# One small operation of block 2's heads, and the copies of the second inverse, get another place in the order

## The chip, the cores and the metric

The kernel runs on one core of a Trainium2 chip. The metric is the device time of one execution in microseconds (us), the median of several runs. Traces come from one profiled execution each. TensorE is called PE, VectorE DVE, ScalarE ACT, GpSimd POOL and SyncE SP; SP issues nearly all DMAs of this kernel, from one queue in order.

## The reference

Two transformer-like blocks over 1024 tokens of width 1024, all in float32. Block 1 (an RWKV branch, a short convolution, a pooling branch) is not touched. Block 2 puts 16 learned meta tokens ahead of the 1024, projects the normalized rows, and then has

- a Fourier branch: a two-dimensional transform over time and channels, and a gate;
- a delta-rule branch with 8 heads of 128 channels. Queries, keys and values go through a depthwise convolution of 5 taps and a SiLU. With the running sum `g` of log decays inside a chunk, `decay[c, s] = exp(g[c] - g[s])` for `s <= c`, and `A = strict_lower((beta*k) k^T * decay)`. `T = (1 + A)^-1` is a unit triangular inverse. The state recurrence over the chunks uses `T`, `q`, `k`, `v` and `decay`, forward and backward in time; the output is normalized per head, multiplied by `silu(z)` and projected;
- a hierarchical mixture of experts.

In code, the core of the part that the change touches:

```
a_mat = where(strict, einsum("bhncd,bhnsd->bhncs", k_beta, k) * decay, 0)
t_mat = triangular_solve(eye + a_mat, eye, lower=True, unit_diagonal=True)
qk    = where(lower, einsum("bhncd,bhnsd->bhncs", q, k) * decay, 0)
```

## The kernel before

The 1040 rows of block 2 are the 16 meta tokens (the meta chunk) and 8 chunks of 128 tokens. A matmul in near-float32 precision is three passes (`mm3`, lines 195 to 197) with both operands split into a high and a low part. Weights stream through `WStream.get`: a 512 KB load (line 184), the high part by ACT (line 172), the low part by POOL (line 173).

**The heads.** The loop at the end of the heads' section runs over 8 heads. For each it projects and convolves the keys, queries and values (`channels`: three projections of three pieces each; PE, ACT copies at line 991, five taps at lines 997 and 999, SiLU at line 1000). Between the pieces it runs one step of the previous head's generator `head`, so the small work of head h-1 lies between the projections of head h. That small work, in the order of the code:

- `token_rows`: transposes of keys and queries (lines 1017 and 1027) into PSUM tiles called "m", of which there are two; ACT squares them (line 1029, tile `jk`), DVE sums the squares (line 1030), ACT copies the rows out (line 1033);
- `decay_matrices(h, 0)`: from `gb`, the rows of `g` broadcast to all partitions, eight DVE operations of 128x128 (line 1090: four chunks, two directions), then ACT's exponential (line 1092). The tiles `dm0` and `dm1` have two buffers each;
- `value_rows`: transposes of the values (lines 1055 and 1063), also through "m";
- `gram_meta`: for the meta chunk a 16x16 product (line 1076, into "m"), one small DVE operation on `gb` (line 1078), its exponential on ACT (line 1080), the product of both on DVE (line 1081), a store (line 1082);
- `decay_matrices(h, 1)` for the other four chunks, and `gram` twice (lines 1105 to 1123), whose products are multiplied with the decays and stored for the inverses.

`decays_in(h)` loads `gb` for both directions (line 1006, 576 KB each, two buffers each) from the scratch `GR`, which `gates_b` has written from a DVE copy (line 974) and a store (line 975).

**What sets the order.** The kernel is traced in the order of the code; a planner then simulates it with estimated durations and puts each engine's instructions into a fixed order: of those that its simulation says are ready, the ones traced earlier first. On the chip each engine follows its order and waits at semaphores. `tc.issue_after(ins)` gives every instruction traced in its block on `ins`'s engine an edge that puts it behind `ins` in that engine's order; it adds no semaphore, and instructions of other engines in the block get no edge. `rows_of[0]` holds such an instruction: the last `GR` copy of `gates_b`, behind which each head's `decay_matrices(h, 0)` stands.

**The inverses.** Behind the heads DVE solves two triangular inverses of 128 matrices of 64x64 (lines 421 and 423), the second one backwards (`solve1`, in place in the tile named `tab`), interleaved with the Fourier branch and its gates. `z_gate(h)` projects the gate of a head and applies SiLU (line 1190, two halves). `inverse_out` stores the inverse (line 1230) and, in four copies by ACT (line 1233, two buffers) with a store each (line 1234), its transpose. After that come nine halves of `gate_d` (line 1373) and the loop over the chunks, which reads both.

Of the kernel before, what the change touches and what calls it, by code (L numbers as in the profile page):

```python
# [17 lines left out]
OP = mybir.AluOpType  # L18
# [109 lines left out]
def tile_kernel(tc, A):  # L128
    with ExitStack() as ctx:
        body(ctx, tc, A)  # L130


def body(ctx, tc, A):
    nc = tc.nc
    act, dve, pool_e, pe, sp = nc.scalar, nc.vector, nc.gpsimd, nc.tensor, nc.sync
# [148 lines left out]
    with ExitStack() as ca:  # L284
# [30 lines left out]
        for pr in range(4):  # L315
# [6 lines left out]
            for half in range(2):  # L322
# [36 lines left out]
                def c8(x):  # L359
# [10 lines left out]
                                         op0=OP.mult, op1=OP.mult)  # L370
# [13 lines left out]
                for g in range(2):  # L384
# [5 lines left out]
                    c = half * 8 + 4 * g  # L390
# [8 lines left out]
                for g in range(2):  # L399
                    c = half * 8 + 4 * g  # L400
# [52 lines left out]
    with ExitStack() as ci:  # L453
        pi = sb("pi", 1, ci)
        X = pi.tile([P, 64, 64], F32, name="X")
        t = pi.tile([P, 1024], F32, name="t")
# [22 lines left out]
    with ExitStack() as cs:  # L479
# [4 lines left out]
        for c in range(16):  # L484
# [38 lines left out]
            if c % 2 == 1:  # L523
                i = c // 2
# [91 lines left out]
    for dt in range(4):  # L616
# [8 lines left out]
        for half in range(2):  # L625
# [3 lines left out]
            for i in range(2):  # L629
                dve.scalar_tensor_tensor(y[half], cu[:, i + t0:512 + i + t0], cw[:, i, dt:dt + 1], y[half],  # L630
                                         op0=OP.mult, op1=OP.add)
# [244 lines left out]
    def con2(name):  # L876
        o, n = cols2.at[name]
        return C2[:, o:o + n]
# [14 lines left out]
    gc = c2.tile([P, 2, 9, H], F32, name="gc")  # L893
# [18 lines left out]
    with ExitStack() as cg:  # L912
# [66 lines left out]
        KQs_, vs_, sks, gbs, silus, rows_of = {}, {}, {}, {}, [None], [None]  # L979
# [92 lines left out]
        def gram_meta(h):  # L1072

            KQ, gb = KQs_[h], gbs[h][0]
            q = psm.tile([P, 4, P], F32, name="m")
            pe.matmul(q[:16, 0, :16], KQ[:, 0, 0:16], KQ[:, 0, 0:16], start=True, stop=True)
            dm = pg.tile([16, 16], F32, name="dmm", bufs=4)
            dve.scalar_tensor_tensor(dm, gb[:16, 0, :16], gc[:16, 0, 0, h:h + 1],
                                     con2("dmf")[:16, :16], op0=OP.subtract, op1=OP.min)
            act.activation(dm, dm, AF.Exp)  # L1080
            dve.scalar_tensor_tensor(dm, q[:16, 0, :16], nbp[:16, 0, 0, h:h + 1], dm, op0=OP.mult, op1=OP.mult)
            sp.dma_start(NM[h], dm)

        def decay_matrices(h, gq):
            grb, dm = gbs[h], []
            for d_ in range(2):
                t = pg.tile([P, 4, P], F32, name=f"dm{d_}", bufs=2)
                for i in range(4):
                    c = 1 + 4 * gq + i
                    dve.scalar_tensor_tensor(t[:, i], grb[d_][:, c, :], gc[:, d_, c, h:h + 1],  # L1090
                                             con2("dmf" if d_ == 0 else "dmb"), op0=OP.subtract, op1=OP.min)
                act.activation(t, t, AF.Exp)
                dm.append(t)
            return dm

        def gram(h, gq, dm):
# [30 lines left out]
        def head(h):  # L1127
            yield from token_rows(h)
            with tc.issue_after(rows_of[0].ins):
                dm0 = decay_matrices(h, 0)  # L1130
            yield from value_rows(h)
            gram_meta(h)
            yield
            dm1 = decay_matrices(h, 1)
            yield from gram(h, 0, dm0)
            yield from gram(h, 1, dm1)
# [49 lines left out]
    def z_gate(h):  # L1186
        w = win2.get(3584 + h * P)
        for half, tt in enumerate(HALF):
            t = pz.tile([P, 512], F32, name="z")
            gated[0] = act.activation(t, half2(w, half), AF.Silu)  # L1190
            sp.dma_start(Z2[h * P:(h + 1) * P, tt], t)
# [37 lines left out]
    def inverse_out(d_, X):  # L1229
        sp.dma_start(TS2[d_], X)  # L1230
        for i in range(4):
            t = pi.tile([P, 16, 64], F32, name="t", bufs=2)
            act.activation(t, X[:, :, 16 * i:16 * i + 16].rearrange("p s t -> p t s"), AF.Copy)
            sp.dma_start(TN2[d_, :, 16 * i:16 * i + 16, :], t)
# [88 lines left out]
    ones(X1_)  # L1323
    for h in range(5, H):
        z_gate(h)
        if h == 5:
            with tc.issue_after(gated[0].ins):
                inverse_out(1, X1_)
    cpi.close()
# [313 lines left out]
    with ExitStack() as ce:  # L1643
# [133 lines left out]
        for half in range(2):  # L1777
            if half:
                ready += [expert_raw(e, whole(weo, 2), parts=early) for e in range(2)]
                for _ in delta_half(1, big, pf, 2):  # L1780
                    if later:
                        i, f = later.pop(0)
# [41 lines left out]
    with ExitStack() as ce:  # L1824
# [11 lines left out]
        for i in range(2):  # L1836
            t = pm.tile([P, D], F32, name=f"xg{i}", bufs=1)
# [357 lines left out]
```

## Time and profile before

| | |
|---|---|
| median of 3 runs | 3046.23 us (3042.31 to 3051.17) |
| profiled execution | 3044.02 us, span 3042.3 us |
| mean granted PE clock | 0.964 |
| PE busy | 2781.8 us (91%), 16109 matmuls |
| weight loads (PEld) busy | 2230.4 us (73%) |
| DVE busy | 1518.0 us (50%) |
| ACT busy | 1027.7 us (34%) |
| POOL busy | 888.6 us (29%) |
| block 2's heads | about 1250 to 1613 us |
| inverses, Fourier branch, gates | about 1613 to 1960 us |

A line of a timeline gives the start in us, the duration in us, the engine, the source line, the operation, output and inputs with shapes, the count, and in brackets how long the engine had been idle before it and what ended that wait. "q" and "m" are PSUM tiles. The granted clock is a share of the full 2.4 GHz. What ended a wait is inferred from semaphores, the last to come being named.

### The profile page before, as it was taken

The page shows a single profiled execution, that of the slowest core. Times are in us where ns is not written, and L with a number is a line of the kernel's source. Part 1 is how long each engine was busy: PE and PEld are TensorE (multiplying, and loading weights), DVE is VectorE, ACT ScalarE, POOL GpSimd, SP SyncE. Part 2 cuts the span into 40 slices and gives each one's busy share as a digit, 9 for nine tenths or more (in the row PEclk, how much of TensorE's full clock was granted, in tenths as well). Part 3 has the DMA queues.
Part 4 walks back from the last instruction along what each step waited for, and adds up shares of the span by engine and source line. Part 5 has one row for each costly group of instructions (what it writes and reads, how often), then busy time and mean ns, then how long its engine had stood idle before and what let it go on. Part 6 is the DMA issues. An engine that isn't in the chain of part 4 may idle for free. (4 is left out here: it accounts for less than half of the span.)

```text
span 3042.3 us, 42743 instructions
## 1 busy us (share of the span) xinstructions
PE 2781.8 (91%) x16109; PEld 2230.4 (73%) x16109; DVE 1518.0 (50%) x2516; ACT 1027.7 (34%) x1837; POOL 888.6 (29%) x703
## 2 busy tenths in 40 slices
PE   7999999999999998798999999999999986888884
PEld 6777877888788787798898778789888753545442
DVE  3343993324411345565677989633564442222226
ACT  5444112223322334565673222244543210111112
POOL 1333223223233552111114852222475310111011
PEclk9999999999999999999999999999999988999997
DMA  4456514544244354466553334599988569999996
GB/s 119 122 141 181 181 42 142 153 134 131 80 137 149 120 149 123 106 154 142 140 145 118 117 94 136 160 275 260 264 248 296 195 248 401 416 404 412 400 370 281
DMA packets 532929, 599.77 MB, mean 197 GB/s; under 512 B 120784, under 2 KB 429188, under 8 KB 512368
## 3 DMA queue, kind: packets, MB, share of 16 engines
q1 hardware_dynamic: 525808, 582.60, 59.2%
q0 software_dynamic: 6912, 14.41, 1.3%
q8 instruction: 128, 2.10, 0.3%
q14 instruction: 81, 0.66, 0.1%
HBM read 473.23 MB, written 134.44 MB: 200 GB/s over the span
## 5 line engine op out<-in xcount | busy, mean ns | idle before, releaser
L173 POOL TENSOR_TENSOR wl<-wr,wh 128x1024 fp32r<-128x1024 f32 x142 | 367.0, 2585 | 632.0 <-ACT wh L172 624.0
L196 PE MATMUL q<-hTh,wl 128*128 128x512 f32 x1040 | 412.8, 397 | 8.0 <-POOL wl L173 8.0
L195 PE MATMUL q<-hTh,wh 128*128 128x512 f32 x1040 | 416.3, 400 | 2.3 <-DVE t L824 1.4
L197 PE MATMUL q<-hTl,wh 128*128 128x512 f32 x1040 | 416.7, 401 | 0.0
L195 PE MATMUL q<-h2h,wh 128*128 128x346 f32 (+4 forms) x1080 | 389.2, 360 | 5.9 <-ACT wh L172 3.4
L196 PE MATMUL q<-h2h,wl 128*128 128x346 f32 (+4 forms) x1080 | 383.3, 355 | 1.6 <-POOL wl L173 1.6
L197 PE MATMUL q<-h2l,wh 128*128 128x346 f32 (+4 forms) x1080 | 381.3, 353 | 0.0
L196 PEld LDWEIGHTS q<-hTh,wl 128*128 128x128 f32 x1040 | 196.6, 189 | 57.7 <-POOL wl L173 9.5
L195 PEld LDWEIGHTS q<-hTh,wh 128*128 128x128 f32 x1040 | 196.6, 189 | 50.4 <-issue 5.8
L197 PEld LDWEIGHTS q<-hTl,wh 128*128 128x128 f32 x1040 | 196.7, 189 | 46.3 <-issue 3.9
L195 PEld LDWEIGHTS q<-h2h,wh 128*128 128x128 f32 (+1 forms) x1080 | 206.7, 191 | 26.6 <-ACT wh L172 3.8
L196 PEld LDWEIGHTS q<-h2h,wl 128*128 128x128 f32 (+1 forms) x1080 | 206.3, 191 | 20.6 <-POOL wl L173 2.1
L197 PEld LDWEIGHTS q<-h2l,wh 128*128 128x128 f32 (+1 forms) x1080 | 205.8, 191 | 18.4 <-issue 0.2
L438 DVE TENSOR_TENSOR t<-X 128x62 f32<-128x62 f32 (+30 forms) x124 | 155.5, 1254 | 10.8 <-DMA br<-in_w_branch_dram 7.7
L172 ACT ACTIVATE wh<-wr 128x1024 fp32r<-128x1024 f32 x142 | 148.5, 1046 | 36.2 <-PE q L197 16.8
L440 DVE TENSOR_TENSOR X<-X,t 128x62 f32<-128x62 f32 (+30 forms) x124 | 151.0, 1218 | 2.8
L1843 POOL DMA_INDIRECT xg<-HN,gidx x28 | 28.6, 1022 | 373.6 <-PE t L1856 313.4
L1862 PE MATMUL q<-yl,xT 128*32 128x256 f32 (+2 forms) x416 | 107.4, 421 | 26.3 <-DMA yl<-in_w_gate_e_dram 26.0
L1864 ACT ACTIVATE sg<-q 128x256 f32<-128x256 f32 x28 | 10.8, 384 | 325.2 <-PE q L1862 325.2
L1862 PE MATMUL q<-mh,xT 128*64 128x256 f32 (+2 forms) x416 | 107.0, 417 | 11.8 <-DMA mh<-in_w_gate_e_dram 11.5
L1865 DVE TENSOR_TENSOR sg<-sg,q 128x256 f32<-128x256 f32 x28 | 11.8, 421 | 211.1 <-ACT sg L1864 211.1
L1862 PE MATMUL q<-g,xT 128*32 128x256 f32 (+2 forms) x400 | 88.0, 449 | 25.4 <-DMA g<-in_w_gate_e_dram 23.4
(631 smaller groups left out, 5890.8 us busy)
## 6 DMA issues: line engine op xcount, KB each, us to landing
wr<-in_w_in_dram SPq DMA_DIRECT2D x125, 512.0 KB, 4.7
d<-in_w_down_e_dram SPq DMA_DIRECT2D x38, 1024.0 KB, 17.6
g<-in_w_gate_e_dram SPq DMA_DIRECT2D x25, 1024.0 KB, 20.0
u<-in_w_up_e_dram SPq DMA_DIRECT2D x25, 1024.0 KB, 17.7
KQ<-KQs SPq DMA_DIRECT2D x32, 512.0 KB, 7.2
KV<-KVs SPq DMA_DIRECT2D x32, 512.0 KB, 6.2
wr<-in_w_gate_e_dram SPq DMA_DIRECT2D x26, 512.0 KB, 18.7
mh<-in_w_gate_e_dram SPq DMA_DIRECT2D x13, 1024.0 KB, 13.7
```

The costliest lines, as they stand in the source:

```text
L172: act.activation(hi, src, AF.Copy)
L173: pool_e.tensor_sub(lo, src, hi.bitcast(F32))
L195: pe.matmul(out, sh(k), mh(k), start=(k == 0), stop=False)
L196: pe.matmul(out, sl(k), mh(k), start=False, stop=False)
L197: mm[0] = pe.matmul(out, sh(k), ml(k), start=False, stop=(k == kt - 1))
L438: dve.tensor_tensor(t, X[:, 0:s, s:s + 1].to_broadcast([X.shape[0], s, m]), X[:, s:s + 1, s + 1:n].to_broadcast([X.shape[0], s, m]), op=OP ...
L440: dve.tensor_add(X[:, 0:s, s + 1:n], X[:, 0:s, s + 1:n], t)
L1843: nc.gpsimd.indirect_dma_start(out=xg, out_offset=None, in_=HN, in_offset=bass.IndirectOffsetOnAxis(ap=gi, axis=0), bounds_check=S - 1, oo ...
L1862: up[0] = pe.matmul(qs[r_, j], xT[:, k, r_], w[j][k], start=(k == 0), stop=(k == 7))
L1864: si[0] = act.activation(sg, qs[:, 0], AF.Silu)
L1865: dve.tensor_mul(sg, sg, qs[:, 1])
```

## The change

Two edits. First, the small DVE operation of `gram_meta` stands behind the last large decay operation traced before it, which is the eighth of `decay_matrices(h, 0)`. For that, `decay_matrices` now writes its last operation into `rows_of[0]`; so the block around `decay_matrices(h, 0)` in `head` stands, from the second head on, behind the last operation of `decay_matrices(h-1, 1)`, no longer behind the `GR` copy. Second, `inverse_out(1, X1_)` is traced in the last turn of the gates' loop, after `z_gate(7)`, and its ACT copies stand behind that gate's second SiLU; before, it was traced after `z_gate(5)` and behind that gate's.

```diff
-            dve.scalar_tensor_tensor(dm, gb[:16, 0, :16], gc[:16, 0, 0, h:h + 1],
-                                     con2("dmf")[:16, :16], op0=OP.subtract, op1=OP.min)
+            with tc.issue_after(rows_of[0].ins):
+                dve.scalar_tensor_tensor(dm, gb[:16, 0, :16], gc[:16, 0, 0, h:h + 1],
+                                         con2("dmf")[:16, :16], op0=OP.subtract, op1=OP.min)
             act.activation(dm, dm, AF.Exp)
...
                 for i in range(4):
                     c = 1 + 4 * gq + i
-                    dve.scalar_tensor_tensor(t[:, i], grb[d_][:, c, :], gc[:, d_, c, h:h + 1],
-                                             con2("dmf" if d_ == 0 else "dmb"), op0=OP.subtract, op1=OP.min)
+                    rows = dve.scalar_tensor_tensor(t[:, i], grb[d_][:, c, :], gc[:, d_, c, h:h + 1],
+                                                    con2("dmf" if d_ == 0 else "dmb"), op0=OP.subtract, op1=OP.min)
                 act.activation(t, t, AF.Exp)
                 dm.append(t)
+            rows_of[0] = rows
             return dm
...
         z_gate(h)
-        if h == 5:
+        if h == 7:
             with tc.issue_after(gated[0].ins):
                 inverse_out(1, X1_)
```

## Rows read from the trace of the kernel before

**Rows 1.** Waits of PE, 1180 to 1620 us: total, times, longest.
```profile
PE m L1063 <- ACT jk L1029: 36.0, 6, 11.7
PE m L1027 <- DVE jk L974: 5.8, 1, 5.8
```
**Rows 2.** Waits of all engines, 1300 to 1600 us.
```profile
DVE dmm L1078 <- DMA gb<-GR: 54.6, 5, 12.0
```
**Rows 3.** Timeline of DVE, around one stalled head.
```profile
1313.22 1.14 DVE L1090 SCALAR_TENSOR_TENSOR dm<-gb,gc,C 128x128 f32<-128x128 f32 x4
...
1330.25 0.22 DVE L1078 SCALAR_TENSOR_TENSOR dmm<-gb,gc,C 16x16 f32<-16x16 f32 x1 [10.23 <-DMA gb<-GR]
...
1339.29 0.22 DVE L1081 SCALAR_TENSOR_TENSOR dmm<-m,nbp,dmm 16x16 f32<-16x16 f32 x1 [1.61 <-PE m L1076]
...
1397.80 2.20 DVE L1090 SCALAR_TENSOR_TENSOR dm<-gb,gc,C 128x128 f32<-128x128 f32 x8
```
**Rows 4.** Timeline of ACT, the same head.
```profile
1330.51 0.21 ACT L1080 ACTIVATE dmm<-dmm 16x16 f32<-16x16 f32 x1 [7.14 <-DVE dmm L1078]
```
**Rows 5.** Timeline of PE, the same head.
```profile
1332.65 0.94 PE L1063 MATMUL m<-ident,v 128*128 128x128 f32 x4 [4.92 <-ACT jk L1029]
...
1333.68 0.49 PE L196 MATMUL q<-h2h,wl 128*128 128x346 f32 x1
...
1336.61 0.32 PE L195 MATMUL q<-h2h,wh 128*128 128x346 f32 x1
```
**Rows 6.** Busy time by stretch, cut at decay groups; stretch, length, engines, clock, DMA share, GB/s.
```profile
1303.03:1350.62 47.59, 42.66 (x261) 41.60 (x260) 29.97 (x68) 30.90 (x50) 8.88 (x10) 0.96 0.67 148
1350.62:1397.80 47.18, 42.71 (x261) 41.59 (x261) 29.97 (x68) 30.93 (x50) 8.88 (x10) 0.96 0.61 147
1397.80:1445.17 47.37, 42.70 (x258) 41.64 (x257) 29.98 (x68) 30.38 (x50) 8.90 (x10) 0.93 0.62 146
1445.17:1493.28 48.11, 43.29 (x264) 42.20 (x263) 30.15 (x69) 31.24 (x51) 8.92 (x10) 0.93 0.57 144
1493.28:1541.82 48.54, 43.09 (x263) 41.98 (x263) 29.99 (x68) 31.33 (x51) 8.90 (x10) 0.93 0.59 143
1541.82:1581.90 40.08, 40.08 (x257) 39.28 (x256) 30.52 (x67) 28.95 (x49) 8.89 (x10) 1.00 0.51 138
1249.80:1312.01 62.21, 44.77 (x267) 43.36 (x266) 33.48 (x83) 31.74 (x56) 7.62 (x10) 0.89 0.49 129
```
**Rows 7.** Timeline of DVE, heads 0 to 2.
```profile
1257.98 0.22 DVE L1078 SCALAR_TENSOR_TENSOR dmm<-gb,gc,C 16x16 f32<-16x16 f32 x1 [6.89 <-DMA gb<-GR]
1258.13 0.27 DVE L974 COPY jk<-m 72x128 f32<-72x128 f32 x1
...
1274.75 0.88 DVE L1090 SCALAR_TENSOR_TENSOR dm<-gb,gc,C 128x128 f32<-128x128 f32 x3 [7.58 <-DMA gb<-GR]
```
**Rows 8.** Timeline of SP's queue, heads 0 to 2.
```profile
1249.86 5.27 SPq L184 DMA_DIRECT2D wr<-in_w_in_dram  x1
...
1265.62 7.04 SPq L1006 DMA_DIRECT2D gb<-GR  x3
```
**Rows 9.** Timelines of ACT and PE, heads 0 to 2.
```profile
1277.56 0.63 ACT L1092 ACTIVATE dm<-dm 128x512 f32<-128x512 f32 x1 [0.42 <-DVE dm L1090]
1283.85 0.21 ACT L1080 ACTIVATE dmm<-dmm 16x16 f32<-16x16 f32 x1 [5.66 <-DVE dmm L1078]
...
1284.93 1.12 PE L1063 MATMUL m<-ident,v 128*128 128x128 f32 x4 [11.66 <-ACT jk L1029]
```
**Rows 10.** Instructions of lines 1190 and 1233; then PE's timeline behind the copies.
```profile
L1190 ACT ACTIVATE z<-q x16: 580/598/605, 1648.2 to 1915.3; 128x512 f32<-128x512 f32 x16
...
L1233 ACT ACTIVATE t<-tab x4: 1911/2010/2054, 1946.6 to 1956.7; 128x1024 f32<-128x1024 f32 x4
...
1951.98 0.79 PE L195 MATMUL q<-h2h,wh 128*128 128x512 f32 x1 [3.40 <-ACT wh L172]
...
1954.39 0.80 PE L196 MATMUL q<-h2h,wl 128*128 128x512 f32 x1 [1.62 <-POOL wl L173]
```

## Prediction

> **What bounds the kernel now.** I began with the granted clock and the page's forty slices: TensorE (PE) is busy for nine tenths of nearly every slice, so a change is worth what it does to PE's few gaps. The waits of PE over block 2's heads name them: two causes, the value transposes of line 1063 six times (36.0 us, the longest 11.7) and one transpose of line 1027 (5.8) [rows 1]. PE is said to wait there for ScalarE's squares (line 1029), which says who came last, not why. The timelines of the other engines say why. VectorE stands still before the meta chunk's decay operation (line 1078), 54.6 us in five heads, until the load of the row-broadcast decays `gb` lands [rows 2]. For head 3: VectorE finished reading the buffer's former contents in the group at 1313.22, the next load could only then start, and the meta operation reached the front of VectorE's queue 10.23 us before that load had landed at 1330.25 [rows 3]. ScalarE had its exponential (line 1080) at the front of its own queue and idled 7.14 us, until 1330.51 [rows 4]. The squares and PSUM copies behind it could not release the two "m" buffers, so PE idled 4.92 us before 1332.65, and then ran a matmul of 346 columns in 0.49 us where it takes 0.32 at the higher clock, until about 1336.6 [rows 5].
>
> The urgent reader of `gb` is thus the smallest one. The 128x128 decay operations of the same head come at 1397.80 for head 3 (eight of them, the first half of the head's decays), 67 us after its `gb` had landed [rows 3].
>
> **First edit, heads 3 to 7.** Afterwards the meta operation stands behind the last large decay operation of its own head's first half, which reads the same `gb`. Nothing is added to the work: 0.22 us on VectorE and its exponential on ScalarE move. The price of the stall is read from a natural comparison. Cut the trace at the start of each head's first eight decay operations, and each stretch is one head's period. Five periods hold one stalled meta operation each (heads 3 to 7) and last 47.59, 47.18, 47.37, 48.11 and 48.54 us. The sixth holds none, because there is no ninth head whose meta operation could stand there, and lasts 40.08 us with PE busy for all of it at clock 1.00 [rows 6]. The differences are 7.51, 7.10, 7.29, 8.03 and 8.46, in all 38.4 us. They split into PE idle (span minus busy: 4.93, 4.47, 4.67, 4.82, 5.45; 24.3) and PE busier than 40.08 by 2.58 to 3.21 (14.1), which is the lower clock after each gap.
>
> Is the sixth period fair as a model? It has no `gb` loads. The DMA share of the five is 0.57 to 0.67 of 47.2 to 48.5 us, at most 31.9 us of the DMA engines' time, which in 40.08 us is a share of 0.80: it fits. I take no loss; as a bound I take the spread of the five periods, 1.4 us, for each of five, 7 us.
>
> Who is late next: in the sixth period nobody before PE. VectorE is busy 30.5 and ScalarE 29.0 of 40.08 us, and the moved 0.22 us goes beside PE. The meta product (line 1081) needs the moved result only at 1339.29 for head 1, whose first eight decay operations began at 1303.03 (the first cut); so the result still comes over 30 us early [rows 3, 6].
>
> The edit also resets the handle that the next head's first decays are ordered behind (once the copy of `GR`, now the second half of the head before). In the trace they stand in that order already: head 1's second half ends near 1314.4, head 2's first half starts at 1350.62, where the second stretch is cut [rows 3, 6]. Cost 0.
>
> **First edit, heads 0 to 2.** Here the stall is mixed with the start of the stage. From the first value-convolution tap of head 0 to that of head 1 takes 62.21 us [rows 6], 22.1 above 40.08. Meta 0 waits until 1257.98 for the first `gb`, and behind it the copy for the second direction's `GR` runs only at 1258.13 [rows 7]. Without the meta operation that copy runs some 7 us sooner, but the next thing on VectorE, head 0's large decays, waits for the same load. SP was still issuing a weight load from 1249.86 for 5.27 us, and the second direction's loads could only go at 1265.62, to be waited for until 1274.75 [rows 7, 8]. I count nothing for this, since that load cannot be shown to come earlier. What surely goes is meta 2: ScalarE finished its large exponentials at 1278.2 (1277.56 plus 0.63) and then idled 5.66 us until the meta's exponential at 1283.85; PE's 11.66 us gap ended at 1284.93, a square and a copy later [rows 9]. PE can resume 5.7 us sooner. Bounds: 0 (the load is later still) and 22.1 (the whole excess). I take 5.7, because it is one instruction's wait read from its row, while the rest hangs on loads.
>
> **Second edit.** The copies of the second inverse are to follow the eighth gate's second Silu. In the trace they do: the last of the 16 Silus starts at 1915.3, the first of those four copies at 1946.6 [rows 10]. The planner has put them behind three activations of the next gate as well, and they wait for VectorE's solve. The edge asks for nothing new. Their trace position falls behind the weight splits, loads and Silus of two gates that all run earlier anyway. What lies on the SP queue behind the inverse's own store is in the same order. So 0. Bounds: if the copies did move, PE's gap of 3.40 + 1.62 us, in which the weight split waits behind the first copies, could go (gain 5.0); or the four copies of 2.01 us each (8.0) could come late for the chunk loop that reads them (loss 8.0).
>
> **The sum.** 38.4 + 5.7 + 0 = 44.1 us off the profiled execution's 3044.0 (span 3042.3) is 2999.9. That execution lies 2.2 below the median of the three runs, 3046.2, so the forecast on that footing is 3002. I take the work behind the heads to move earlier as a block.
>
> **Rivals.**
> 1. *Only the idle time returns.* PE at full duty would keep the lower clock for as many matmuls. Gain 24.3 + 5.7 = 30.0, time 3016. Against it: the sixth period, 40.08 us busy throughout, shows 1.00, and the slow matmuls of head 3 follow its gap [rows 5, 6]. The Trainium skill ("TensorE: Matmul & The Clock Gate", Part 1: The HAM clock gate) says that for a model the penalty of the clock's ramp is under 1% of a typical kernel's span; left out on that ground, it gives this rival's sum. So it is here too as a share of the span, but it is 14.1 of the 38.4 us that these heads can give back, too much to leave out. Chance 0.08.
> 2. *The wait passes on.* With the meta operation gone, another reader of `gb` comes to the front while the load is under way, or the planner, which knows nothing of the real landing time, pulls another operation there. Time about 3046. For it: one large decay operation did wait, at 1274.75 [rows 7]. Against: from head 3 on they come 67 us after the landing, since their own output buffers hold them back until the products before them are done. Chance 0.06.
> 3. *More than counted.* The start of the stage runs at the sixth period's pace and the gap at the copies closes: 38.4 + 22.1 + 5.0 = 65.5, time 2981. For it: the earlier `GR` copy. Against: the loads it feeds stand behind others. Chance 0.07.
> 4. *Slower.* The meta product frees one of the two "m" PSUM buffers, and now depends on the large decays through VectorE's order. If the planner lets PE's meta matmul go before those decays, PE loses a buffer until they are done: from a meta product at 1339.29 to the end of the next decay group (1350.62 and eight operations of about 0.28, 1352.8) is 13.5 us, for eight heads 108, less the 44.1 saved: 64 slower, 3110. It begins where the decays come after their head's meta matmul; for head 1 they come over 30 us before its product, and the code writes them before it. Chance 0.05.
>
> **How the numbers follow.** The forecast has 0.74. Its own range is 2992 to 3012: 7 us for the DMA bound, and the runs' own spread of about 5 each way. To hold 8 in 10 I reach to rival 1 and part of the way to rival 3: 2986 to 3020. A difference under 0.3% (9 us) can't be told from none. Faster: forecast, rivals 1 and 3, 0.89. Same: rival 2, 0.06. Slower: rival 4, 0.05.
>
> **What would show it.** Right: line 1078 no longer waits for `gb` in VectorE's waits; PE has no gap at line 1063 in heads 3 to 7; every period between first decay groups is 40 to 41.5 us at clock 1.00; near the start one PE gap remains, ending at the large exponentials; the copies of the second inverse start about 45 us earlier with the same gap on PE. Wrong: a period above 43 us, or a new reader of `gb` at the front of VectorE's queue; a PE wait on the buffer of line 1076; the stretch from the heads to the chunk loop longer or shorter by more than 5 us.

## The result, and the profile after

The median went from 3048.7 to 3017.4 us, 31.3 us less: ratio 0.9895, 95% interval 0.9857 to 0.9933. The forecast, 3002, was 15 us too low. The time lies inside the stated range, 2986 to 3020, and outside the forecast's own, 2992 to 3012. The profiled execution after is the quickest of its four, 3005.9 us, 38.2 under the one before. The heads' stage, from the first start of line 967 to the last meta product, went from 368.7 to 338.2 us, 30.5 less. It began 1.2 us earlier, and what lies behind it took 1424.7 us, not 1431.2. That last stretch varies from 1424.7 to 1440 us over the profiles shown here, whatever was changed in the heads, so the stage is the better measure of the effect. It is one profile of each kernel, though: the kernel with the first edit alone, below, has the same order in the heads, and there the stage took 334.3 us, 34.4 less, and the median fell by 35.5. The effect is thus some 30 to 35 us.

Lines behind the edit have moved by one or two: the meta operation is line 1079, its product 1082, the large decays 1091 with the exponential in 1093, the masked products 1112 (`at`), SiLU of `z` 1192, the copies of the second inverse 1235.

Waits of PE after, 1180 to 1620 us (total, times, longest):

```profile
PE m L1063 <- ACT jk L1029: 7.7, 6, 2.1
PE q L196 <- POOL cl L173: 5.5, 1, 5.5
PE m L1055 <- ACT jk L1029: 4.5, 1, 4.5
PE m L1027 <- ACT kv L1033: 3.4, 1, 3.4
```

Against [rows 1], 36.0 us at line 1063 have become 7.7, of which 5.6 in five heads; the 5.5 of the second line lie behind the heads. The waits of all engines after, 1250 to 1580 us, say what stands behind the rest:

```profile
ACT dm L1093 <- DVE dm L1091: 52.7, 29, 7.5
DVE at L1112 <- DMA OFF<-at: 30.0, 14, 4.6
DVE dm L1091 <- DMA gb<-GR: 17.1, 2, 10.7
```

The 54.6 us of [rows 2] are gone: no meta operation waits for `gb`. The 17.1 belong to the first two heads alone. New is the middle line: DVE waits 14 times for a store to have read `at`, which has one buffer; in 1300 to 1600 us this wait came to 3.6 us in 7 times before and to 31.3 in 15 after.

The windows after, cut as [rows 6] at each head's first decay group (stretch, length, then PE, PEld, DVE, ACT and POOL busy, granted clock, DMA share, GB/s):

```profile
1296.99:1339.01 42.02, 42.02 (x267) 41.13 (x266) 30.64 (x69) 29.23 (x49) 8.87 (x10) 1.00 0.77 171
1339.01:1381.33 42.32, 41.61 (x266) 40.52 (x264) 30.61 (x68) 29.19 (x49) 8.84 (x10) 1.00 0.72 162
1381.33:1423.99 42.66, 41.15 (x261) 40.09 (x261) 30.60 (x68) 29.18 (x49) 8.81 (x10) 1.00 0.74 157
1423.99:1467.85 43.86, 42.18 (x259) 40.95 (x258) 30.56 (x68) 29.32 (x49) 8.84 (x10) 0.96 0.78 164
1467.85:1510.05 42.20, 41.83 (x266) 40.74 (x266) 30.65 (x68) 29.19 (x49) 8.87 (x10) 1.00 0.63 165
1510.05:1552.47 42.42, 41.05 (x261) 39.96 (x260) 30.61 (x67) 29.18 (x49) 8.80 (x10) 1.00 0.56 154
```

Periods of 47.2 to 48.5 have become 42.0 to 43.9, not 40.1. The clock is back at 1.00 in all but the fourth, which has the longest idle time. PE still idles 0.4 to 1.7 us (length minus busy) in five of the six. One head shows how. DVE's timeline after (start, duration, operation, and in brackets the idle time before it and what ended it):

```profile
1339.01 2.18 DVE L1091 SCALAR_TENSOR_TENSOR dm<-gb,gc,C 128x128 f32<-128x128 f32 x8
1341.11 0.22 DVE L1079 SCALAR_TENSOR_TENSOR dmm<-gb,gc,C 16x16 f32<-16x16 f32 x1
...
1346.26 0.61 DVE L1112 SCALAR_TENSOR_TENSOR at<-g,nbp,dm 128x128 f32<-128x128 f32 x2 [3.73 <-DMA OFF<-at]
...
1351.49 2.18 DVE L1091 SCALAR_TENSOR_TENSOR dm<-gb,gc,C 128x128 f32<-128x128 f32 x8
```

The meta operation runs behind the large ones without a wait, as intended. But DVE idles 3.73 us at line 1112, so the second half's decays come late, ACT waits for them, and PE waits for ACT's squares. ACT's timeline, and then PE's:

```profile
1352.65 0.63 ACT L1093 ACTIVATE dm<-dm 128x512 f32<-128x512 f32 x1 [2.96 <-DVE dm L1091]
```

```profile
1363.32 0.66 PE L1063 MATMUL m<-ident,v 128*128 128x128 f32 x4 [0.71 <-ACT jk L1029]
```

Why the store is late is read from SP's own queue after, from one head's `gb` loads to the next stores of `at` (the second figure is how long SP needed to issue that one DMA; a wait for a buffer lies ahead of it, as before the weight load at 1363.38, whose buffer POOL had read until 1363.35):

```profile
1356.92 1.67 SPq L1006 DMA_DIRECT2D gb<-GR  x1
...
1360.51 0.74 SPq L1006 DMA_DIRECT2D gb<-GR  x1
1363.38 5.38 SPq L184 DMA_DIRECT2D wr<-in_w_in_dram  x1
1368.86 4.53 SPq L1058 DMA_DIRECT2D KV<-kv  x1
...
1380.79 2.86 SPq L1122 DMA_DIRECT2D N<-at  x1
```

Behind the two loads SP needs 2.9 to 5.4 us for the issues shown, and it is still behind when the stores of `at` are due, 23.9 us after the first load's issue. In the kernel without the loads, below, none of SP's 208 issues between 1300 and 1580 us took more than 1.32 us; here 30 of 213 take more than 1.5. SP's queue before:

```profile
1317.76 2.36 SPq L1006 DMA_DIRECT2D gb<-GR  x2
1320.21 5.59 SPq L1034 DMA_DIRECT2D KVs<-kv  x1
1325.89 2.97 SPq L184 DMA_DIRECT2D wr<-in_w_in_dram  x1
...
1348.35 0.59 SPq L1120 DMA_DIRECT2D N<-at  x1
```

There, too, the issues behind the loads are slow. But 30.6 us lay between the first load and the store, since every head lost 7 us, and SP had caught up by then.

At the start of the stage, DVE after, against [rows 7]:

```profile
1249.82 0.27 DVE L974 COPY jk<-m 72x128 f32<-72x128 f32 x1
1256.53 2.19 DVE L1091 SCALAR_TENSOR_TENSOR dm<-gb,gc,C 128x128 f32<-128x128 f32 x8 [6.43 <-DMA gb<-GR]
...
1273.79 1.14 DVE L1091 SCALAR_TENSOR_TENSOR dm<-gb,gc,C 128x128 f32<-128x128 f32 x4 [10.65 <-DMA gb<-GR]
```

The `GR` copy runs 8.3 us sooner, but the second direction's loads are issued only 1.0 us sooner (1264.62 against 1265.62), since SP needs 5.12 us for the weight load ahead and 5.95 for the `GR` store itself. PE after has three smaller gaps where [rows 9] has one of 11.66, beside the 5.8 of [rows 1]:

```profile
1260.41 1.11 PE L1027 MATMUL m<-ident,KQ 128*128 128x128 f32 x4 [3.36 <-ACT kv L1033]
...
1276.13 0.38 PE L1055 MATMUL m<-ident,v 128*16 128x128 f32 x1 [4.52 <-ACT jk L1029]
...
1278.62 1.12 PE L1063 MATMUL m<-ident,v 128*128 128x128 f32 x4 [2.11 <-ACT jk L1029]
```

And the second edit, the copies of the inverse in the groups of tile `t`, then PE's timeline beside them:

```profile
L1235 ACT ACTIVATE t<-tab x4: 1917/1987/2049, 1916.3 to 1926.4; 128x1024 f32<-128x1024 f32 x4
```

```profile
1921.68 0.80 PE L195 MATMUL q<-h2h,wh 128*128 128x512 f32 x1 [3.38 <-ACT wh L172]
...
1924.11 0.80 PE L196 MATMUL q<-h2h,wl 128*128 128x512 f32 x1 [1.63 <-POOL wl L173]
```

The last Silu starts at 1885.0; the copies come 31.3 us behind it in both kernels, with the same gap on PE, 3.38 + 1.63 against 3.40 + 1.62 [rows 10].

### The profile page after: what moved, and what is told of

Read it like the earlier page. It is cut to its first block, busy times and chain, and to the rows that moved or that the text cites. A ratio compares the mean times of both kernels' runs of the same rounds, so it can differ in the third digit from the quotient of the medians.

```text
span 3004.1 us, 42737 instructions
## 1 busy us (share of the span) xinstructions
PE 2773.0 (92%) x16109; PEld 2222.2 (74%) x16109; DVE 1522.4 (51%) x2516; ACT 1018.3 (34%) x1832; POOL 885.8 (29%) x703
## 5 line engine op out<-in xcount | busy, mean ns | idle before, releaser
L438 DVE TENSOR_TENSOR t<-X 128x62 f32<-128x62 f32 (+30 forms) x124 | 152.3, 1228 | 10.7 <-DMA br<-in_w_branch_dram 7.1
```

The source lines that it names most:

```text
L438: dve.tensor_tensor(t, X[:, 0:s, s:s + 1].to_broadcast([X.shape[0], s, m]), X[:, s:s + 1, s + 1:n].to_broadcast([X.shape[0], s, m]), op=OP ...
```

## The experiments

The theory: DVE and ACT work in a fixed order, and a small early operation that waits for a slow load (`gb`, 14 us in the median) holds up all that is queued behind it. Reordering takes that away; what stays is that the same loads crowd the other DMAs. The rivals are named in each expectation. Each result gives the median, that of the kernel before measured beside it, and the ratio with its 95% interval. "Distance" is the time from one head's meta product to the next.

**One edit alone.** The change with its first edit only:

```diff
-        if h == 7:
+        if h == 5:
             with tc.issue_after(gated[0].ins):
                 inverse_out(1, X1_)
```

> The first edit alone (the second inverse's copies again traced behind the sixth gate). Theory: the second edit asks for what the planner had done anyway, so this is the changed kernel: the same order on every engine and a time within 6 us of it, 28 to 40 us below before; the copies start as many us after the last gate's Silu as in the changed kernel (31 us). Rival: the second edit has a share of the gain, 5 us or more, and this kernel lacks it.

3008.97 against 3044.44: ratio 0.9893 (0.9879 to 0.9907), that of the whole change. Every engine's instructions stand in the same order as in the whole change (two neighbouring matmuls of line 1864 apart), so the second edit does nothing, in the plan as in the time. Its first six distances sum to 251.6 us, where the changed kernel's sum to 254.4; so far do two profiles of one order differ. Its waits repeat those above:

```profile
DVE at L1112 <- DMA OFF<-at: 26.0, 14, 4.3
```

**Without the loads.** Heads 2 to 7 read the tiles of heads 0 and 1 and load none of their own (their decays are thus another head's), once with the meta operation early, as before, and once with it late, as after:

```diff
-            gbs[h] = []
-            for d_ in range(2):
+            gbs[h] = gbs[h - 2] if h > 1 else []
+            for d_ in range(2 if h < 2 else 0):
```

> The kernel before, with one thing taken out: heads 2 to 7 make no gb load of their own and use the tiles of heads 0 and 1 (their decays are then those of the wrong head). The meta operation keeps no edge. Theory: the stall is the wait for the gb load at the front of VectorE's queue. Without loads the meta operations of heads 2 to 7 wait for nothing, PE has no gap of 4.5 to 5.5 us at line 1063, the distances between the meta products of heads 1 to 6 fall from 47.2 to 48.2 us to 41 to 42 us, and the time falls by 30 to 42 us against before. Rival: something else of a head's period holds PE, and the load only came last: periods stay above 45 us and the time falls by less than 12 us.

3016.18 against 3046.9: 0.9898 (0.9884 to 0.9913), a gain of 30.7 with the old order. So the waits did come from the loads. But its meta operation, pulled forward, then waited for something else, the store of its own result's buffer, with one distance of 45.05:

```profile
DVE dmm L1078 <- DMA NM<-dmm: 24.8, 4, 8.6
```

> The changed kernel with the same thing taken out (no gb loads from head 2 on, decays of the wrong head). Theory: the changed kernel's heads last 42.0 to 44.0 us and not 40.9 because the gb loads now share a shorter period with the stores, so that the stores of at come late and VectorE waits for them (30.0 us in 14 waits), then ScalarE for the decays and PE for the squares. Without the loads these waits fall below 8 us, PE's waits at line 1063 from 5.6 us in five heads to under 2, the periods fall to 40.5 to 41.5 us, and the heads take 7 to 10 us less than in the changed kernel. Rival: the order that the planner gave the changed kernel is what costs: waits for at and periods of 42 us and more stay, and the heads take within 3 us of the changed kernel's.

3008.08: 0.9879 (0.9864 to 0.9893). The distances are 40.93 and five times 40.89, then 39.76 for the last. Waits and one window (cut as above) of this kernel:

```profile
DVE at L1112 <- DMA OFF<-at: 7.3, 8, 3.4
```

```profile
1380.02:1420.91 40.89, 40.89 (x262) 40.06 (x261) 31.25 (x69) 29.92 (x50) 8.89 (x10) 1.00 0.52 141
```

Two things follow. 40.89 us is a head's period with PE never idle at the full clock. And with the loads the late stores of `at` go, and PE's waits at line 1063 in the heads with them: the heads' stage, 330.0 us, is 8.2 us shorter than after the change and 4.3 shorter than with the first edit alone. The medians don't show this much apart (a gain of 38.8 us against 35.5, with intervals that overlap). The run takes away the loads' traffic together with their place in SP's queue; it can't say which of the two the stores felt.

**A small load for the meta operation.** On the kernel before, the meta operation reads a 1 KB load of its own, so that it needn't wait for `gb`:

```diff
+            gm = pg.tile([16, 16], F32, name="gm", bufs=4)
+            sp.dma_start(gm, GR[0].rearrange("(o c h) t -> o h c t", o=1, h=H)[:, h, 0, 0:16].broadcast_to([16, 16]))
-            dve.scalar_tensor_tensor(dm, gb[:16, 0, :16], gc[:16, 0, 0, h:h + 1],
+            dve.scalar_tensor_tensor(dm, gm, gc[:16, 0, 0, h:h + 1],
```

> The kernel before, but the meta operation reads a 16x16 tile of its own, loaded by a small DMA of 1 KB, in place of gb; no edge. Theory: what costs is that a small operation waits for the large load in an in-order queue, wherever it stands. Then this gains as the change does: 25 to 42 us against before, no meta wait above 3 us from head 3 on. Rival: the small load waits behind the large ones on the same queue, so the meta operation waits nearly as long as before: meta waits of 5 us and more stay, and the gain is under 12 us.

3041.82 against 3046.9: 0.998 (0.9971 to 0.9988). Every number of the theory missed; the rival's came true, waits of over 5 us and a gain of under 12, but not for its reason. The planner, seeing an early input, pulled the meta operations further forward, until they met the four buffers of their own result:

```profile
DVE dmm L1080 <- DMA NM<-dmm: 42.0, 4, 12.9
```

The waiting instruction had another reason and the same place, and so most of the cost stayed: it is a wait at that place in an in-order queue that costs, whatever is waited for. With eight buffers of `dmm` and `gm` that reason goes too:

```diff
-            dm = pg.tile([16, 16], F32, name="dmm", bufs=4)
-            gm = pg.tile([16, 16], F32, name="gm", bufs=4)
+            dm = pg.tile([16, 16], F32, name="dmm", bufs=8)
+            gm = pg.tile([16, 16], F32, name="gm", bufs=8)
```

> The kernel with the meta operation's own 16x16 load (early in VectorE's queue, no edge), with eight buffers of its result instead of four, so that a meta operation need not wait for the store of the one four heads before (42.0 us in four waits there). Theory: the place in the queue is what costs, any wait of the early operation will do: with nothing left to wait for, it costs nothing, the distances between the meta products of heads 1 to 6 are 41 to 43 us, and the time is 25 to 40 us below before. Rival: the stalls of that kernel had another cause; the periods of 47 to 50 us stay and the gain stays under 12 us.

3024.05 against 3044.44: 0.9932 (0.9918 to 0.9946), 20.4 us, under the 25 to 40 expected. All eight meta operations are done by 1266.8 and none waits in the heads. The first six distances are 40.3 to 43.7 us but for one of 47.0. What is left by its waits is one long stall of PE and a wait for DVE's products:

```profile
PE m L1063 <- ACT jk L1029: 9.9, 1, 9.9
...
PE g L1107 <- DVE qt L1114: 9.1, 4, 3.0
```

**The loads in another place of the queue.** On the changed kernel, each `gb` load behind the one before it in SP's order:

```diff
+                if gbs_of[0] is None:
+                    ld = sp.dma_start(gb, ...
+                else:
+                    with tc.issue_after(gbs_of[0].ins):
+                        ld = sp.dma_start(gb, ...
+                gbs_of[0] = ld
```

> The changed kernel, with the gb loads put in the order of the heads on SP's queue: both of head 0 before those of head 1. Theory for the start of the stage: VectorE waits 10.65 us for head 0's second gb because head 1's first lies before it on the queue. Then that load lands 4 to 7 us earlier, the wait falls to 4 to 7 us, PE's gaps before the value transposes of head 0 shrink, and the time falls by 3 to 8 us against the changed kernel. Rival: the second direction's rows (GR) are written too late, since SP's queue is held by a weight load: the wait stays near 10 us and so does the time.

3013.52 against 3046.9: 0.9894 (0.988 to 0.9909), not told apart from the change. The load came sooner, as the theory has it: DVE waits 3.95 us for head 0's second `gb`, not 10.65. But head 0's product comes only 2.5 us earlier behind the stage's start (41.9 against 44.4), and the next distance, 44.14, gives it back. DVE's wait for `at` is as after the change, 28.2 us. Instead PE waits 4.9 us at the meta matmul. So the wait for the second load is not worth its length in time, and the order of the loads among themselves is not what makes the stores late.

**The loads from another queue.** GpSimd issues them, so that no store stands behind them on SP:

```diff
-                sp.dma_start(gb, ...
+                pool_e.dma_start(gb, ...
```

> The changed kernel with the gb loads issued by GpSimd on its own queue. Theory: the stores of at come late because they stand on SP's queue behind the loads' transfers; on another queue they pass them. VectorE's waits for at (30.0 us) fall below 12 us, periods to 40.9 to 41.6 us, the time by 4 to 10 us against the changed kernel. Rival: all queues share the same 16 DMA engines and what is late is the work on them: the waits stay above 20 us, the time within 3 us of the changed kernel's or worse, since GpSimd now issues between its weight splits.

3019.62 against 3044.44: 0.9921 (0.9908 to 0.9935). The wait for `at` did fall, over the same stretch to 3.2 us in 4, as the theory has it. But the time is 10.7 us over that of the first edit alone, measured beside it, and the distances are 43.4 to 45.7 until the sixth. What backs up now are other stores, on a queue in which no `gb` load stands. SP's queue behind a pair of loads that GpSimd issues at 1351.97, and the waits:

```profile
1355.18 3.46 SPq L1038 DMA_DIRECT2D KQs<-KQ  x1
1358.73 6.69 SPq L184 DMA_DIRECT2D wr<-in_w_in_dram  x1
1365.52 6.48 SPq L1034 DMA_DIRECT2D KVs<-kv  x1
...
1384.63 0.58 SPq L1122 DMA_DIRECT2D N<-at  x1
```

```profile
POOL gb L1006 <- DVE dm L1091: 16.2, 5, 4.0
ACT kv L1067 <- DMA KVs<-kv: 14.7, 4, 6.2
PE m L1076 <- ACT kv L1067: 10.3, 5, 3.4
```

When the stores of `at` come, the burst is over; the stores of `kv` are late instead, ACT waits for them and PE for ACT. Of SP's 186 issues between 1300 and 1580 us 17 take more than 1.5 us, the longest 8.3. So SP's issues need not stand behind the loads in one queue to be slow, against the theory; that all queues share the DMA engines, as the rival has it, fits. It is no clean test of the queue, since the loads' packets changed too: GpSimd's ten loads were 1,600 packets for 5.90 MB, 3.7 KB on average, where SP's are of 512 bytes. A median `gb` landed in 14.3 us (15.5 in the same stretch after the change). The Trainium skill ("DMA: Bandwidth & Descriptors", Issuing engines are not separate DMA queues) says that DMAs started by several engines run on the same DMA engines, and that starting them elsewhere saves only the starting engine's time. The trace agrees: the landing is nearly the same, and SP's issues are slow all the same, though the time to issue, up to 8.3 us, is not small here.

Both together:

```diff
-                    ld = sp.dma_start(gb, ...
+                    ld = pool_e.dma_start(gb, ...
```

> The last one with the loads also in the order of the heads. Theory: the two gains add, as the one is in the heads from 1 on and the other at the start of the stage: 3 to 5 us less than with the loads by GpSimd alone. Rival: the order of the loads no longer matters on a queue of their own, since the second direction's rows (GR) come late: within 2 us.

3029.97: 0.996 (0.9946 to 0.9973). Worse again, by 10 us, and neither the theory's number nor the rival's. Head 0's product comes 9.5 us later behind the stage's start (49.6 against 40.2), and `PE m` waits for ACT's `kv` 16.5 us in 6.

**The loads made quicker.** `gb` is a partition's nine rows of 512 bytes, which in `GR` lie eight rows apart. With `GR` written in the order of heads they are one run of 4608 bytes:

```diff
-                sp.dma_start(GR[d_], gr)
+                sp.dma_start(GR[d_].rearrange("(h c) t -> c h t", h=H), gr)
...
-                sp.dma_start(gb, GR[d_].rearrange("(o c h) t -> o h c t", o=1, h=H)[:, h].broadcast_to([P, 9, P]))
+                sp.dma_start(gb.rearrange("p c t -> p (c t)"), GR[d_].rearrange("(o h c) t -> o h (c t)", o=1, h=H)[:, h].broadcast_to([P, 9 * P]))
```

> The changed kernel, with the scratch GR stored head by head, so that a gb load reads one run of 4608 bytes for each partition in place of nine of 512; every engine's order stays as it is. Theory: what is left of the loss is DMA work that crowds the stores; the loads land in 5 to 9 us (now 9.7 to 17.0), VectorE's waits for at fall from 26 to 30 us to under 12, the distances between meta products to 40.9 to 41.5 us, the time by 5 to 12 us against the changed kernel. Rival: the loads' time goes by bytes, not by runs: landing times, waits and time stay within 20%, 20% and 3 us.

On the changed kernel: 2989.31 against 3043.21, 0.9818 (0.9805 to 0.9831), a gain of 53.9 us. By the updates of their semaphores, 16 to a load, the 16 loads landed in 9.1, 14.9 and 18.8 us (least, median, most) after the change and in 4.3, 6.9 and 8.5 here, for the same 576 KB. The program's DMA packets fell by 16,390, which is about 128 partitions times eight rows for each of 16 loads. Its SP queue at the place shown above, and a window:

```profile
1340.60 1.40 SPq L1006 DMA_DIRECT2D gb<-GR  x1
...
1342.63 0.57 SPq L1006 DMA_DIRECT2D gb<-GR  x1
1347.16 0.37 SPq L184 DMA_DIRECT2D wr<-in_w_in_dram  x1
1351.74 0.33 SPq L1058 DMA_DIRECT2D KV<-kv  x1
...
1364.08 0.59 SPq L1122 DMA_DIRECT2D N<-at  x1
```

```profile
1366.36:1407.26 40.90, 40.90 (x262) 40.08 (x261) 31.24 (x68) 29.95 (x50) 8.91 (x10) 1.00 0.60 170
```

The stores come 23.5 us behind the first load's issue, as after the change, but SP issues what comes behind the loads in 0.3 to 0.6 us, DVE's wait for `at` is down to 8.1 us in 9, and PE never stops. That is 18 us over the first edit alone (35.5), where 5 to 12 were expected. Against that kernel's trace, 6.5 us are the six distances (251.6 to 245.1) and 13.8 the start of the stage, to head 0's product (43.3 to 29.5), which I had not counted. The Trainium skill ("DMA: Bandwidth & Descriptors", Why small descriptors are slow) gives a fixed cost of about 3 cycles beside one cycle per 32 bytes of a packet. By that, nine packets of 512 bytes cost 171 cycles and one of 4608 costs 147, and 14.9 us would become 12.8 (an estimate from that page). The direction agrees; the measured 6.9 is far below.

The same loads with the old order:

> The kernel before with the same contiguous loads and the meta operation still early. Theory: the stall is as long as the load takes to land after the buffer came free; with the loads landing 5 to 8 us sooner, PE's gaps at line 1063 in heads 3 to 7 (4.5 to 5.5 us) close, the distances fall from 47 to 48 us to 41 to 43, and the time falls by 25 to 45 us without the change. Rival: the loads land no sooner; distances above 45 us, a gain under 10 us.

2996.71: 0.9852 (0.9835 to 0.9869), 46.5 us without the change at all. The early meta operation still waits for `gb`, 25.9 us in 6 where it was 54.6 in 5, the longest 5.6; of that PE feels 2.6 us at line 1063. Beside quick loads the change is worth 7.4 us by the medians, 3.2 by the heads' stage of the two profiles (317.6 and 314.4).

With the order of x6 as well:

> The changed kernel with contiguous loads and both gb loads of head 0 ahead of those of head 1. Theory: the second direction's gb lands earlier at the start of the stage as well, so this is 2 to 6 us below the changed kernel with contiguous loads alone. Rival: with short loads their order no longer matters: within 2 us of it.

2986.58: 0.9811 (0.9798 to 0.9825). The best here, under both kernels, and within the interval of the run with the loads alone.

## Why the prediction was right, and where it was too high

The direction and the mechanism held: the early operation's wait for `gb` was what cost, and moving it took that away. Of the 44.1 us the heads gave 30.5, and 34.4 in the profile of the first edit alone.

- **The stall of heads 3 to 7, counted 38.4, measured 27.0** (29.4 with the first edit alone). Two errors. The model period was short: cut at product lines, the five stalled distances of before sum to 238.9 us, and five of 40.89 to 204.5, which leaves 34.5. The decay groups move against PE's work, so the sixth period of [rows 6], 40.08, held 257 matmuls where a head has 261 or 262; its own row showed it. That is 3.9 us. It sits in the term put down to the clock: with 261 matmuls to each stretch PE's idle time is 24.3 us, as counted, and the busy time above 40.89 is 10.2, not 14.1. The failed step is the other: "it fits. I take no loss." A DMA share of 0.80 does fit as a mean, and the windows after show 0.56 to 0.78; but the loads come in a burst, and SP's issues back up behind it. The five distances after lie 7.5 us above five of 40.89, and 5.1 with the first edit alone; the sixth, which had no stall before, went from 40.9 to 42.4. Both runs that take the burst away, without loads and with quick ones, stand at 40.89. The bound of 7 is about this size, though it was taken from the spread of the old periods and not from the loads.
- **Meta 2 and the start, counted 5.7, measured 4.8.** From the stage's start to head 0's product 49.2 us became 44.4. What I refused to count, an earlier second load, indeed moved by 1.0 us only; but three PE gaps stay, not one.
- **The second edit, counted 0, is 0**, shown by the run without it. The copies came 30 us earlier, not 45, because the block moved by what the heads gave.
- **The handle, counted 0.** Nothing in the traces speaks against it; it was not run by itself.
- **The range.** It holds 3017.4 only because it was stretched up to rival 1, only the idle time, whose 3016 is near the median by chance. That rival's mechanism did not come: the clock is back at 1.00 in five windows, and the loss lies in waits. So in part the range held by luck; with the first edit alone's gain, 35.5, the time would have been in the forecast's own range too.
- **The other rivals.** **Rival 2**, the wait passes on, was true in part: not to another reader of `gb`, but to the stores issued after the loads. **Rival 3** didn't come: the start stayed slow, and the quick loads show that up to 15 us lay there. **Rival 4**: PE has no wait at the meta matmul after.
- **Its own signs.** The meta operation waits for `gb` no more, and the gap at the copies of the inverse is the same. But line 1063 still has five gaps of 0.4 to 1.6 us in the heads, no period is within 40 to 41.5 us, and one, 43.86, is above the 43 that was to show it wrong.

Not settled: how much a second buffer of `at` would save was not tried, nor what makes nine rows cost twice one run. The number of packets alone is not it, since GpSimd's packets of 3.7 KB landed about as late. The loads do hold the DMA engines longer: by the window rows (share times length, an estimate) a head's DMAs take 21.3 us of the 16 engines without loads, 24.5 with the quick ones and 30.5 to 34.2 in the first four windows after.

## What to carry to other kernels

When a small operation at the front of an in-order queue waits, ask what is queued behind it, and move it, rather than feed it otherwise: with another input the planner pulled it into the next wait. Then look at the load itself; one run per partition in place of nine was worth more here than the whole reordering. And take a floor period from the engine that bounds it, cut at that engine's work, with its instructions counted, and ask of a mean DMA share what comes in one burst, and which issues fall into it, on whatever queue.

## What the runs showed of the hardware that was not expected

- The same 576 KB broadcast to 128 partitions landed in 6.9 us (median of 16 loads) as one run per partition and in 14.9 as nine runs of 512 bytes.
- SP took at most 1.32 us for any of 208 issues in the heads without such loads, and up to 6.9 with them, so a store of 64 KB could be late though the DMA engines were busy for only 0.56 to 0.78 of the time. With the loads issued by GpSimd SP still took up to 8.3.
- PE gaps of 0.4 to 1.5 us, one to a head, left the granted clock at 1.00; the one of 1.6 stood in the period with 0.96. Gaps of about 5 us in the kernel before went with 0.93 to 0.96.
